# Latent attention: the scores of both softmax maps in one PSUM tile of three banks, and two PSUM tiles for the neighbourhood scores

## The chip, the cores and the metric

One Trainium2 chip, one of its cores. The metric is the device time of one execution of the whole program in microseconds (us); lower is better. The kernel before takes 2817.27 us, the median of three runs (2814.94 to 2818.51).

## What is computed

The program is a network of two blocks over 512 tokens of width 1024. The change is in the second block, which has two layers. In each layer a part of the token width goes through two kinds of attention, with 4 heads of 64 each: a neighbourhood attention (`neighbourhood_attention`: every token sees a window of 8 rows by 16 columns and 256 context tokens) and a latent differential attention, which uses two softmax maps over 512 + 256 keys and subtracts one from the other:

```python
def diff_attend(q1, q2, k1, k2, v, lam):
    scale = DIFF_QK_DIM ** -0.5
    s1 = jnp.einsum('bqhd,bkhd->bhqk', q1, k1).astype(jnp.float32) * scale
    s2 = jnp.einsum('bqhd,bkhd->bhqk', q2, k2).astype(jnp.float32) * scale
    p = jax.nn.softmax(s1, axis=-1) - lam * jax.nn.softmax(s2, axis=-1)
    return jnp.einsum('bhqk,bkhd->bqhd', p.astype(v.dtype), v)
```

`diff_latent` calls it with k1 and k2 made of the 512 rotated keys of the tokens and 256 keys of the context, one block of 128 queries at a time. In the first layer the 256 context tokens also attend to themselves, with 256 keys.

## The kernel before

The kernel is written with a tile framework: the Python code names tiles, and a scheduler decides the order of the instructions on each engine from the program's order and its own costs, and puts in the waits. That order is fixed when the program is built. TensorE (PE), VectorE (DVE), ScalarE (ACT) and the queues of SP and POOL each run their instructions in order.

`attention` (L1653) is one stage per layer. It opens the SBUF tags, replaces the PSUM tags of the matrix products (`GEMM_PS`) by `SOFT_PS`, and runs `units` (L1618): for each of 4 heads and each of 4 query blocks (qb) one neighbourhood unit and one differential unit, 16 pairs a stage. What a unit leaves for later (transposes of the probabilities and the product with the values, `attend_values`, L1409) is run two units later (`AHEAD = 2`). [...] `SOFT_PS` gives `s2` two tiles of 768 columns, which take two banks each, `s1` one tile of one bank, `po` one bank (the products with the values) and `tr` two (transposes).

A differential unit (`differential`, L1501) does for each of two maps: the scores, as two matmuls of 512 and 256 columns into an `s2` tile (L1513); the max over 768 columns on DVE (L1514); the exponential on ACT, which also sums (L1515, recorded under the helper's line L135, tile `ne` for map 0 and `wl` for map 1); the reciprocal of the sum on DVE (L1516). Then DVE combines the maps over 768 columns into `ne` (L1520, helper line L145).

A neighbourhood unit (`neighbour`, L1427) writes 256 columns of context scores into the `s1` tile (L1441, L1442), takes their minimum on DVE (L1445), writes 256 columns of window scores (L1451, L1452), adds the bias and takes the minimum on DVE (L1454), and takes the exponential of 512 columns on ACT (tile `f`, L135).

`attend_values` transposes the probabilities on PE (L1417, tile `tr`), copies them to SBUF (L1421 on ACT, for a part of the neighbourhood units L1419 on DVE) and multiplies with the values on PE (L1423, tile `po`).

In the first layer the same functions also run for the context (`context`, L1642) ahead of the stage, beside matrix products, with 256 keys and the PSUM tag `at` for all scores.

Of the kernel before, what the change touches and what calls it, by code (L numbers as in the profile page):

```python
# [17 lines left out]
P = 128  # L18
# [7 lines left out]
GROUPS = ((128, 1), (512, 4), (2048, 16))  # L26

GEMM_PS = {"mm": 3, "at": 2, "po": 1, "tr": 2}
SOFT_PS = {"s2": 2, "s1": 1, "po": 1, "tr": 2}
BASE = {  # L30
    "wr": 2, "wh": 4, "wl": 4, "f": 5, "h": 2, "acc": 2, "ident": 1, "identr": 1, "ones": 1,
    "rs_y": 4, "rs_t": 2, "rs_v": 2, "rs_v1": 2, "rs_vd": 1, "sil": 2, "adar": 2, "bst": 2, "nb": 2,
# [46 lines left out]
class Net:  # L79
# [1421 lines left out]
    def differential(self, s, yd, ssq, head, qb, qst, kst, vs, c, po):  # L1501
        nc = self.nc
        nk = kst.shape[2]
        cuts = [(k0, min(k0 + 512, nk)) for k0 in range(0, nk, 512)]
        qs = slice(qb * P, (qb + 1) * P)
        sm = self.t([P, 16], "dsm")
        em = []
        for mp in range(2):
            b = mp * 8
            e = self.t([P, nk], self.soft["e"][mp])  # L1510
            ps = self.ps((P, nk), self.soft["s2"])
            for k0, k1 in cuts:
                nc.tensor.matmul(ps[:, k0:k1], lhsT=qst[:, mp, qs], rhs=kst[:, mp, k0:k1], start=True, stop=True)  # L1513
            nc.vector.tensor_reduce(out=sm[:, b + 2:b + 3], in_=ps, axis=AX.X, op=ALU.max, negate=True)  # L1514
            self.act(e, ps, AF.Exp, bias=sm[:, b + 2:b + 3], accum_out=sm[:, b + 3:b + 4])  # L1515
            nc.vector.reciprocal(out=sm[:, b + 6:b + 7], in_=sm[:, b + 3:b + 4])  # L1516
            em.append(e)

        self.stt(sm[:, 15:16], sm[:, 14:15], c["nlam"], sm[:, 3:4], ALU.mult, ALU.mult)
        self.stt(em[0], em[1], sm[:, 15:16], em[0], ALU.mult, ALU.add)  # L1520

        def values():
            o = yd[:, qb, head * 64:(head + 1) * 64]
            self.act(o, self.attend_values(em[0], vs, head, po), scale=sm[:, 6:7])
            junk = self.t([P, 64], "nj")
            self.act(junk, o, AF.Square, accum_out=ssq[:, head, qb:qb + 1])
            if head == 3 and qb == 0 and not s.ctx:
                self.diff_norm(s, yd, ssq, 0, 3)
            if head == 3 and qb == s.nt - 1:
                self.diff_norm(s, yd, ssq, 0 if s.ctx else 3, 4)  # L1530
        return values
# [121 lines left out]
    def attention(self, s, l, c, ne):  # L1653
        self.soft = {"e": ("ne", "wl"), "s2": "s2", "s1": "s1", "pt": "wh"}
        self.open("soft", ne=ne, nsm=5, dsm=5, ssq=2, nj=2)
        self.psum(SOFT_PS)
        po = self.ps((P, 4, P), "po")
        ckv = self.ckv
        vc = [ckv[1][:, i] for i in range(2)]
        vd = [s.kv[3][:, i] for i in range(s.nt)] + [ckv[3][:, i] for i in range(2)]  # L1660
        st, bts = s.st, [self.nbias(l, 0)]

        def more(head):
            bts.append(self.nbias(l, head))
            st.append(self.stacks(s, head))
        todo = [v for v in self.units(s, c, po, st, more, s.kv[1], vc, vd, bts) if v]
        self.gather_start(s)
        for values in todo:
            values()
        self.close("soft")  # L1670
        self.close("heads")
        self.psum(GEMM_PS)
# [249 lines left out]
```

## Time and profile before

| | |
|---|---|
| median of 3 runs | 2817.27 us (2814.94 to 2818.51) |
| profiled execution, its own time | 2815.33 us |
| its span, first to last instruction | 2813.6 us |
| mean granted clock of TensorE | 0.996 of full speed |
| instructions | 38388 |
| first attention stage, from the first scores to the last units | 1452.4 to 1540.9 us of the span |
| second attention stage | 2301.3 to 2388.9 us of the span |

The profile is one execution, recorded by the hardware. All times in it count from the start of its span; the 1.7 us between span and time lie around it. Matmuls are pipelined and their ends are modelled, so the busy time of TensorE is not work at its peak. "PEld" is the loading of a matmul's weights, which runs beside the matmuls before it. Where a helper records an operation, its line is the helper's, so the groups are told apart by their tiles; the profile shows both `s1` and `s2` as `s`.

### The profile page before, as it was taken

To read this page: it belongs to the slowest core of one execution; us is meant where nothing else is said; L and a number is where in the kernel's file an instruction comes from. 1 tells how busy PE (TensorE), PEld (TensorE's weight loads), DVE (VectorE), ACT (ScalarE), POOL (GpSimd) and SP (SyncE) were. 2 spreads that over 40 slices of the span, in tenths; PEclk is the share of its full clock that TensorE was granted. 3 is DMA by queue.
4 is the path that set the end of the run, shared out by engine and by line. 5 is a ranking of instruction groups with operands and counts; after the bars stand their busy time and mean duration, and the time that the engine had idled before them with its cause. 6 is when DMAs were issued, how large, how long until landed. Compare 5 with 4: busy or idle time off the path is not lost.

```text
span 2813.6 us, 38388 instructions
## 1 busy us (share of the span) xinstructions
PE 2750.5 (98%) x15332; PEld 2339.3 (83%) x15332; DVE 1716.7 (61%) x3205; ACT 1057.1 (38%) x1969; POOL 62.4 (2%) x109
## 2 busy tenths in 40 slices
PE   8999999999999999999998999999999999999999
PEld 4888888988888888789887888888888887888887
DVE  6667776453557888787768564444446758644434
ACT  4433433333434222244648232222224547433323
POOL 3000000000020000000000000000000000000000
PEclk9999999999999999999999999999999999999999
DMA  8455344333364555745443411221123443332321
GB/s 275 131 190 173 129 148 141 114 119 105 119 197 135 181 191 192 240 156 174 129 126 79 129 60 60 63 73 61 60 68 106 133 126 90 120 105 90 101 94 60
DMA packets 275203, 354.74 MB, mean 126 GB/s; under 512 B 19320, under 2 KB 221170, under 8 KB 274768
## 3 DMA queue, kind: packets, MB, share of 16 engines
q1 hardware_dynamic: 259744, 323.58, 36.7%
q0 software_dynamic: 4384, 13.99, 1.6%
q10 hardware_dynamic: 10896, 14.72, 1.6%
q8 instruction: 121, 1.98, 0.3%
q14 instruction: 58, 0.48, 0.1%
HBM read 318.62 MB, written 23.65 MB: 122 GB/s over the span
## 4 chain that ended last, share of the span: by engine, by line
PE 82%; DVE 7%; DMA 5%; ACT 3%; issue 2%; POOL 1%; SPq 0%; DVEq 0%; ACTq 0%; POOLq 0%
PE mm L209 24%; PE mm L210 24%; PE mm L211 24%; DMA wr<-in_ada_w 2%; PE po L1423 2%; DVE ada L145 2%; DMA wr<-in_w_ff 2%; DVE wl L138 1%; ACT wh L149 1%; PE at L209 1%; PE tr L1417 1%; PE tr L391 1%; PE at L210 1%; PE at L211 1%; DVE dsm L1514 1%
## 5 line engine op out<-in xcount | busy, mean ns | idle before, releaser
L149 ACT CAST wh<-wr 128x1024 fp32r<-128x1024 f32 (+1 forms) x442 | 425.8, 970 | 842.5 <-PE mm L210 703.8
L138 DVE TENSOR_TENSOR wl<-wr,wh 128x1024 fp32r<-128x1024 f32 (+1 forms) x442 | 494.0, 1122 | 348.6 <-ACT wh L149 339.8
L209 PE MATMUL mm<-h,wh 128*128 128x512 f32 (+1 forms) x1712 | 654.2, 384 | 3.6 <-ACT h L135 2.6
L210 PE MATMUL mm<-h,wh 128*128 128x512 f32 (+1 forms) x1712 | 654.3, 383 | 0.4 <-DVE h L145 0.3
L211 PE MATMUL mm<-h,wl 128*128 128x512 f32 (+1 forms) x1712 | 653.4, 383 | 0.5 <-DVE wl L138 0.5
L209 PEld LDWEIGHTS mm<-h,wh 128*128 128x128 f32 x1712 | 320.9, 188 | 67.6 <-ACT h L135 3.9
L210 PEld LDWEIGHTS mm<-h,wh 128*128 128x128 f32 x1712 | 321.3, 188 | 65.3 <-DVE ada L145 1.7
L211 PEld LDWEIGHTS mm<-h,wl 128*128 128x128 f32 x1712 | 321.6, 188 | 62.6 <-DVE wl L138 0.9
L210 PE MATMUL mm<-mid,wh 128*128 128x512 f32 (+1 forms) x864 | 335.3, 388 | 0.5 <-DVE mid L138 0.5
L209 PE MATMUL mm<-mid,wh 128*128 128x512 f32 (+1 forms) x864 | 335.1, 388 | 0.0
L211 PE MATMUL mm<-mid,wl 128*128 128x512 f32 (+1 forms) x864 | 334.5, 387 | 0.0
L145 DVE SCALAR_TENSOR_TENSOR ada<-wr,cs,ada 128x1024 f32<-128x1024 f32 x168 | 212.6, 1280 | 35.2 <-DMA wr<-in_ada_w 23.9
L135 ACT ACTIVATE f<-mm 128x256 f32<-128x256 f32 (+2 forms) x192 | 99.4, 519 | 260.9 <-PE mm L211 260.6
L209 PE MATMUL mm<-wh,h 128*128 128x256 f32 x704 | 197.4, 281 | 0.0
L210 PE MATMUL mm<-wl,h 128*128 128x256 f32 x704 | 197.2, 280 | 0.0
L211 PE MATMUL mm<-wh,h 128*128 128x256 f32 x704 | 197.0, 280 | 0.0
L210 PEld LDWEIGHTS mm<-mid,wh 128*128 128x128 f32 x864 | 162.5, 188 | 37.1 <-DVE mid L138 1.3
L211 PEld LDWEIGHTS mm<-mid,wl 128*128 128x128 f32 x864 | 162.4, 188 | 36.2
L209 PEld LDWEIGHTS mm<-mid,wh 128*128 128x128 f32 x864 | 162.4, 188 | 35.6
L145 DVE SCALAR_TENSOR_TENSOR x<-mm,modx,x 128x512 f32<-128x512 f32 (+1 forms) x116 | 84.8, 731 | 175.0 <-PE mm L211 172.7
L138 DVE TENSOR_TENSOR f<-f 128x512 f32<-128x512 f32 (+2 forms) x172 | 99.4, 586 | 143.8 <-ACT f L135 142.7
L210 PEld LDWEIGHTS mm<-wl,h 128*128 128x128 f32 x704 | 133.5, 190 | 0.7 <-issue 0.2
(470 smaller groups left out, 4194.0 us busy)
## 6 DMA issues: line engine op xcount, KB each, us to landing
wr<-in_w_ff SPq DMA_DIRECT2D x96, 1024.0 KB
wr<-in_w_in SPq DMA_DIRECT2D x69, 1024.0 KB
wr<-in_ada_w SPq DMA_DIRECT2D x48, 1024.0 KB
wr<-in_w_ada SPq DMA_DIRECT2D x16, 1024.0 KB
wr<-in_w_in SPq DMA_DIRECT2D x24, 512.0 KB
awr<-in_w_ada SPq DMA_DIRECT2D x16, 512.0 KB
wr<-in_w_ret_out SPq DMA_DIRECT2D x8, 1024.0 KB
wr<-in_w_out SPq DMA_DIRECT2D x8, 1024.0 KB
```

The source lines that it names most:

```text
L135: return self.nc.scalar.activation(out=out, in_=in_, func=func, **kw)
L138: return self.nc.vector.tensor_tensor(out=out, in0=a, in1=b, op=op)
L145: return self.nc.vector.scalar_tensor_tensor(out=out, in0=a, scalar=s, in1=b, op0=op0, op1=op1)
L149: self.nc.scalar.copy(hi, src)
L209: mm(out, lhsT=ah, rhs=bh, start=start, stop=False)
L210: mm(out, lhsT=ah, rhs=bl, start=False, stop=False)
L211: mm(out, lhsT=al, rhs=bh, start=False, stop=stop)
L391: when(self.nc.tensor.transpose(ps[:, j], acc[:, m * P:(m + 1) * P], self.ident))
L1417: self.nc.tensor.transpose(tp[:, i], e[:, (b0 + i) * P:(b0 + i + 1) * P], self.ident)
L1423: self.nc.tensor.matmul(po, lhsT=pt[:, kb], rhs=vs[kb][:, head // 2 * P:(head // 2 + 1) * P], start=kb == 0, stop=kb == nk - 1)
L1514: nc.vector.tensor_reduce(out=sm[:, b + 2:b + 3], in_=ps, axis=AX.X, op=ALU.max, negate=True)
```

## The change

`s2` becomes one tile of 1536 columns (three banks), made once a stage and kept in `self.sc`; map 0 has its columns 0 to 767, map 1 the columns 768 to 1535. Map 0's scores are cut at 512, map 1's at 256, so that no matmul crosses a bank: bank 0 holds 512 columns of map 0, bank 1 the last 256 of map 0 and the first 256 of map 1, bank 2 the last 512 of map 1. The bank that this frees goes to a second `s1` tile. The context's own attention keeps its tiles of 256 columns.

```diff
-SOFT_PS = {"s2": 2, "s1": 1, "po": 1, "tr": 2}
+SOFT_PS = {"s2": 1, "s1": 2, "po": 1, "tr": 2}
...
         nk = kst.shape[2]
-        cuts = [(k0, min(k0 + 512, nk)) for k0 in range(0, nk, 512)]
         qs = slice(qb * P, (qb + 1) * P)
...
             e = self.t([P, nk], self.soft["e"][mp])
-            ps = self.ps((P, nk), self.soft["s2"])
+            if s.ctx:
+                ps, cuts = self.ps((P, nk), "at"), ((0, nk),)
+            else:
+
+                ps, cuts = self.sc[:, mp * nk:(mp + 1) * nk], (((0, 512), (512, 768)), ((0, 256), (256, 768)))[mp]
             for k0, k1 in cuts:
...
         po = self.ps((P, 4, P), "po")
+        self.sc = self.ps((P, 1536), "s2")
```

The lines after the first change of `differential` move down by 3 (L1513 becomes L1516, L1514 L1517, L1516 L1519). The scheduler puts the stage in another order. The number behind a tile's name tells one use of it from the next; a name in the waits is the engine whose progress is waited for (Activation is ACT).

On PE, at the scores of the first units of the first stage, before: every map has a tile of its own number, and the tiles 13295 and 13302 (first unit), 13356 and 13363 (second) follow each other in two places in PSUM.

```order
L1513 MATMUL s2_13302<-kst_13127,cqd_13126 128x512 [waits PE_49]
L1513 MATMUL s2_13302<-kst_13127,cqd_13126 128x256
L1451 MATMUL s1_13284<-cqn_13129,cqn_13128 128x256 [waits DVE_49]
L1452 MATMUL s1_13284<-hc_12614,qn_12456 128x256
L1513 MATMUL s2_13356<-kst_13127,cqd_13126 128x512 [waits Activation_49]
L1513 MATMUL s2_13356<-kst_13127,cqd_13126 128x256
L1441 MATMUL s1_13333<-kc_13130,cqn_13128 128x256 [waits Activation_49]
L1442 MATMUL s1_13333<-ckn_11435,qn_12456 128x256
L1417 MATMUL tr_13343<-ident_61,f_13282 128x128 x4
L1513 MATMUL s2_13363<-kst_13127,cqd_13126 128x512 [waits Activation_49]
L1513 MATMUL s2_13363<-kst_13127,cqd_13126 128x256
```

Here the scores of the second unit's map 0 (13356) wait for the exponential of the first unit's map 0, two maps back, and those of its map 1 (13363) for that of the first unit's map 1.

The same engine and place after the change, from the scores of the second unit's map 0 (512, then 256 columns) to those of its map 1 (256, then 512):

```order
L1423 MATMUL po_13277<-hc_12918,wh_13341 128x128 [waits Activation_49]
L1423 MATMUL po_13277<-hc_12918,wh_13341 128x128
L1423 MATMUL po_13277<-cvn_11481,wh_13341 128x128 x2
L1516 MATMUL s2_13278<-kst_13127,cqd_13126 128x512 [waits Activation_49]
L1516 MATMUL s2_13278<-kst_13127,cqd_13126 128x256
L1451 MATMUL s1_13390<-cqn_13129,cqn_13128 128x256 [waits DVE_49]
L1452 MATMUL s1_13390<-hc_12614,qn_12456 128x256
L1451 MATMUL s1_13448<-cqn_13129,cqn_13128 128x256 [waits DVE_49]
L1452 MATMUL s1_13448<-hc_12614,qn_12456 128x256
L1417 MATMUL tr_13369<-ident_61,ne_13295 128x128 [waits DVE_49]
L1516 MATMUL s2_13278<-kst_13127,cqd_13126 128x256 [waits Activation_49]
L1516 MATMUL s2_13278<-kst_13127,cqd_13126 128x512
```

The first wait for Activation at L1516 is for the exponential of the first unit's map 1, the second for that of this unit's map 0: one map back each. The neighbourhood scores (13390 and 13448 are those of the third and fourth units) now come well ahead of their unit.

On DVE, at the third and fourth differential units of the first head after the change (L1519 is the reciprocal, L1517 the max, the last digits of `dsm` name the unit):

```order
L1519 RECIPROCAL dsm_13411<-dsm_13411 128x1 [waits Activation_49]
L1517 TENSOR_REDUCE dsm_13411<-s2_13278 128x1 [waits PE_49]
L1519 RECIPROCAL dsm_13411<-dsm_13411 128x1 [waits Activation_49]
L145 SCALAR_TENSOR_TENSOR dsm_13411<-dsm_13411,lams_9354 128x1 [waits DVE_49]
L145 SCALAR_TENSOR_TENSOR ne_13412<-wl_13418,dsm_13411,ne_13412 128x768 [waits DVE_49]
L1517 TENSOR_REDUCE dsm_13469<-s2_13278 128x1 [waits PE_49]
```

Between the exponential of map 1 (for which the second reciprocal waits) and the max of the next unit stand the reciprocal, the small product and the combination over 768 columns. At the passage to the third unit before the change (unit 13414) the max stood ahead of the combination:

```order
L1516 RECIPROCAL dsm_13354<-dsm_13354 128x1 x2
L1514 TENSOR_REDUCE dsm_13414<-s2_13416 128x1
L145 SCALAR_TENSOR_TENSOR dsm_13354<-dsm_13354,lams_9354 128x1 [waits DVE_49]
L1445 TENSOR_REDUCE nsm_13392<-s1_13393 128x1 [waits PE_49]
L145 SCALAR_TENSOR_TENSOR ne_13355<-wl_13362,dsm_13354,ne_13355 128x768 [waits DVE_49]
```

## Rows read from the trace of the kernel before

**Rows 1.** The page's part 1, whole program: busy us, share, instructions.
```profile
PE 2750.5 (98%) x15332; PEld 2339.3 (83%) x15332; DVE 1716.7 (61%) x3205; ACT 1057.1 (38%) x1969; POOL 62.4 (2%) x109
```
**Rows 2.** Table by stage, both attention stages: length, busy us (instructions), clock, DMA share, GB/s.
```profile
1452.40:1540.90 88.50, 79.53 (x580) 69.72 (x580) 75.74 (x200) 69.27 (x188) 0.00 (x0) 0.98 0.42 101
2301.30:2388.90 87.60, 78.68 (x580) 68.42 (x580) 75.93 (x201) 68.56 (x184) 0.00 (x0) 1.00 0.43 101
```
**Rows 3.** Timeline, start of the first stage: start us, us, instruction, [idle before <-releaser].
```profile
1454.26 0.90 ACT L135 ACTIVATE ne<-s,dsm 128x768 f32<-128x768 f32 x1 [1.70 <-DVE dsm L1514]
...
1455.30 0.30 PEld L1513 LDWEIGHTS s<-kst,cqd 128*128 128x128 f32 x2 [1.69 <-ACT ne L135]
1455.30 0.61 PE L1513 MATMUL s<-kst,cqd 128*128 128x512 f32 x2 [1.48 <-ACT ne L135]
...
1455.95 0.96 DVE L1514 TENSOR_REDUCE dsm<-s 128x1 f32<-128x768 f32 x1 [0.39 <-PE s L1513]
...
1456.21 0.46 PEld L1417 LDWEIGHTS tr<-ident,f 128*128 128x128 f32 x4
...
1456.86 0.67 PE L1513 MATMUL s<-kst,cqd 128*128 128x512 f32 x2
...
1456.95 0.90 ACT L135 ACTIVATE ne<-s,dsm 128x768 f32<-128x768 f32 x1
```
**Rows 4.** Timeline of ACT: last exponential of stage one, first and last of stage two.
```profile
1537.37 0.90 ACT L135 ACTIVATE wl<-s,dsm 128x768 f32<-128x768 f32 x1
...
2303.12 0.90 ACT L135 ACTIVATE ne<-s,dsm 128x768 f32<-128x768 f32 x1 [1.70 <-DVE dsm L1514]
...
2385.43 0.92 ACT L135 ACTIVATE wl<-s,dsm 128x768 f32<-128x768 f32 x1
```
**Rows 5.** Groups by line and shape, 1450 to 1545 us: busy us, mean ns | idle before.
```profile
L1514 DVE TENSOR_REDUCE dsm<-s 128x1 f32<-128x768 f32 x32 | 30.1, 949 | 2.9 <-PE s L1513 2.5
...
L145 DVE SCALAR_TENSOR_TENSOR ne<-wl,dsm,ne 128x768 f32<-128x768 f32 x16 | 16.3, 1016 | 0.3
...
L1421 ACT COPY wh<-tr 128x512 f32<-128x512 f32 x24 | 13.9, 585 | 5.6 <-PE tr L1417 5.6
...
L135 ACT ACTIVATE f<-s,nsm 128x512 f32<-128x512 f32 x16 | 11.0, 685 | 0.3 <-DVE rs_t L138 0.3
...
L1421 ACT COPY wh<-tr 128x256 f32<-128x256 f32 x16 | 6.0, 374 | 2.4 <-PE tr L1417 2.3
L1419 DVE COPY wh<-tr 128x512 f32<-128x512 f32 x8 | 5.5, 685 | 1.0 <-PE tr L1417 1.0
...
L1516 DVE RECIPROCAL dsm<-dsm 128x1 f32<-128x1 f32 x32 | 4.7, 154 | 3.1 <-ACT wl L135 3.0
...
L145 DVE SCALAR_TENSOR_TENSOR dsm<-dsm,lams 128x1 f32<-128x1 f32 x16 | 3.4, 211 | 0.1
```
**Rows 6.** Line L1441 over the whole span: PE's idle time before it (us, times).
```profile
  ACT f L135: 4.0, 10
```
**Rows 7.** Windows, busy us of PE, PEld, DVE, ACT, POOL, then the granted clock, DMA, GB/s.
```profile
1454.00:1455.00 1.00, 0.00 (x0) 0.00 (x0) 1.00 (x4) 0.74 (x1) 0.00 (x0) 1.00 0.86 183
...
1457.00:1458.00 1.00, 1.00 (x5) 0.66 (x5) 0.81 (x3) 1.00 (x3) 0.00 (x0) 0.64 0.86 185
1458.00:1459.00 1.00, 1.00 (x4) 0.90 (x4) 1.00 (x5) 0.86 (x2) 0.00 (x0) 0.50 0.68 146
1459.00:1460.00 1.00, 1.00 (x7) 1.00 (x6) 0.98 (x3) 1.00 (x3) 0.00 (x0) 0.50 0.95 201
1460.00:1461.00 1.00, 1.00 (x7) 0.96 (x6) 0.25 (x2) 0.21 (x2) 0.00 (x0) 0.66 0.35 68
...
2385.00:2390.00 5.00, 3.01 (x23) 2.62 (x24) 4.48 (x9) 2.41 (x8) 0.00 (x0) 1.00 0.50 172
```

## The prediction

> **What bounds the kernel now.** I read the page's busy shares first. Over the whole program TensorE is busy 98% and VectorE 61% [rows 1], but that average is made by the long matrix products, and the change touches only the two attention stages, so the second view is the table by stage [rows 2]. In the 88.5 us of the first stage TensorE is busy 79.5, VectorE 75.7 and ScalarE 69.3 us: 90, 86 and 78%. The second stage (87.6 us) looks the same. No engine rests for long, and none is full. Such a stage is set by how well three queues that each run in order mesh.
>
> The third view is the timeline of one map [rows 3]. A map is one softmax of 128 queries over 768 keys: two matmuls, a max on VectorE, an exponential on ScalarE. Follow one tile: its old exponential ends at 1454.26 + 0.90 = 1455.16; the weight load of the next scores starts at 1455.30; the max starts at 1455.95 and takes 0.96; the exponential starts at 1456.95 and ends at 1457.85. One use of one tile, from exponential end to exponential end, is **2.69 us**. Now there are two tiles: at 1456.86 TensorE writes scores into the one, and 0.09 us later ScalarE starts reading the other. The two 2.69 us chains run beside each other.
>
> The fourth reading is the length of the run of exponentials [rows 3, 4]: from 1454.26 to 1537.37 + 0.90 = 1538.27 is 84.0 us for 32 maps, 2.63 us a map; in the second layer from 2303.12 to 2385.43 + 0.92 = 2386.35 is 83.2 us, 2.60 a map. With two tiles a map may take 5.4 us and the pace still holds, so each map has about 2.6 us in hand to wait in a queue.
>
> **What the change does to this.** It adds and removes no work: 32 maps of 768 columns and 16 neighbourhood units of 512 columns a stage, on the same engines. It cuts the pairs of matmuls of map 1 into 256 and 512 columns instead of 512 and 256, which costs nothing (the same columns). What moves is the waits. Both maps now live in one tile, and the order of TensorE shows it: in the new program the first matmul of map 1 waits for the exponential of map 0 of the same unit, and the first matmul of map 0 of the next unit waits for the exponential of map 1. So one chain runs through all 32 maps of a stage where two ran side by side. Queued behind each such wait on TensorE are transposes and value products; VectorE's max and then ScalarE wait for it.
>
> *The chain alone.* 31 steps of 2.69 plus a last exponential of 0.90 are 84.3 us, against 84.0 and 83.2 now: **+0.3 and +1.1 us**. By itself the chain would just hold the pace. But the 2.6 us in hand are gone, and whatever delays a step now delays the end.
>
> *VectorE's queue.* When an exponential of map 1 ends, VectorE has to do the reciprocal (0.154), the small product (0.211) and the combination of the two maps over 768 columns (1.016) [rows 5]. TensorE needs 0.79 us in the same time for the next scores (1455.16 to 1455.95, [rows 3]). Where the next max stands ahead of the 768-column combination, nothing is lost. Counting the new order of VectorE, at 8 of the 15 passages from unit to unit the combination stands ahead of the max, and at 5 of these a 512-column copy (0.685, [rows 5]) does too. The max then starts 1.38 or 2.07 us after the exponential instead of 0.79: 3 x 0.59 + 5 x 1.28 = **8.2 us a stage**. Three of the eight have a further short instruction in the way; I leave that out against the 0.1 us by which neighbouring instructions overlap in these rows. Today the same order stands in places and costs less, as the max is a tile ahead there.
>
> *ScalarE's queue.* After the exponential of map 0, ScalarE copies the transposed probabilities of an earlier unit (512 columns 0.585, 256 columns 0.374, [rows 5]) before the exponential of map 1. Those transposes stand on TensorE behind the scores of map 1, which wait for the exponential. So the first copy starts after 0.79 plus the four weight loads of the transposes (0.46 for four, [rows 3]), about 1.2 us, and the second ends at 2.15; the max is done at 0.79 + 0.96 + 0.04 = 1.79. The step grows by 0.36. In the new order of ScalarE I count 11 such steps a stage (4.0 us), and three more, after an exponential of either map, where one or two neighbourhood exponentials (0.685) are in the way as well, which I put at 0.8 each: **6.4 us a stage**. This is the least certain term; nothing now shows it. Its lower end is zero (copies may overlap a max that is late anyway), its upper end 16 x 0.96 = 15 us (both copies in full in every step).
>
> *The neighbourhood tiles.* Two tiles let the scores of two or more units run ahead. What that can give is bounded by what TensorE now idles for this tile: 4.0 us over both stages [rows 6]. I cost it at zero: the chain of the maps sets the end, and work done early for the neighbourhood only fills queues earlier. After the last exponential the same instructions follow as now. If the cover were gone, it would be 4 us for the change.
>
> *Sum.* First stage 0.3 + 8.2 + 6.4 = 14.9, second 1.1 + 8.2 + 6.4 = 15.7, together 30.6 us. The profiled execution took 2815.3, so it would take 2845.9. The median of the three runs shown, 2817.3, is 1.9 above it: **2848 us**.
>
> The row of the order has the 512-column matmul of map 0 wait for the exponential of map 1, though the two touch different banks. [...]
>
> **The rivals.**
>
> *The clock falls (chance 0.13).* TensorE will be busy some 80 of 99 us instead of 80 of 88. [...] Against it: in 2385 to 2390 TensorE was busy only 3.01 of 5 us and the clock stayed at 1.00 [rows 7]. [...]
>
> *The queues mesh anyway (chance 0.10).* Only one of the two queue terms shows, because a late max gives the copies time. Then 1.4 + 2 x 8 = 17 us: about 2834.
>
> *Not slower (chance 0.07).* The place is the passage from exponential to next scores. Neighbourhood scores that ran ahead leave VectorE and ScalarE free when the chain wants them, and each step keeps 2.69 us. Then the stages cost +1.4 less up to 4.0 of the neighbourhood's idle time: 2815 to 2819. The point where it decides is the delay per step: below 0.1 us (31 x 0.1 x 2 = 6 us) nothing could be told from no change. For it: VectorE's 75.7 us of work would fit into 84. Against it: the combination of 1.016 us stands in the way at 8 places by the order alone.
>
> *The change does not do what it says.* If the two maps' banks let both chains run beside each other still, there would be no slowdown. The waits in the order exclude it; I give it no chance of its own beyond the last case.
>
> **How the numbers follow.** Forecast as summed, 0.67, own range 2838 to 2860; the clock 0.13; half the queue terms 0.10; not slower 0.07; something unseen, on the high side, 0.03. A range from 2830 to 2870 leaves out the not-slower case, most of the clock's and what is unseen: about 0.2. A change of 0.2%, 5.6 us, is about what a measurement of this kernel can tell from none. Faster by more needs the whole neighbourhood gain and a chain without delays: 0.02. Within 0.2%: 0.05. Slower: 0.93.
>
> **What would show it.** In the profile after, the run of 32 exponentials should take 97 to 101 us a stage. Idle time of TensorE before the scores of a map should name exponentials of the other map and grow from the present few us to over ten, and VectorE's max should wait for TensorE more often. VectorE's share of the stage should fall to about 76%, durations of single instructions staying. Everything outside the two stages should keep its length. The step on VectorE is wrong if the max follows 0.8 us after the exponential at nearly all passages; the step on ScalarE is wrong if it idles before the exponentials of map 1. The prediction is wrong altogether if the run of exponentials stays under 87 us, or if the scores of the next map start before the exponential of the other has ended. A granted clock of 0.9 or less over the stages would mean the first rival.

## The result, and the profile after

The changed kernel takes 2857.37 us, the median of four runs (2850.89 to 2857.78); the kernel before took 2816.55 in the same comparison. The ratio is 1.0141, with a 95% interval of 1.0129 to 1.0154: **slower by 40.8 us**. The profiled execution took 2850.89 us with a span of 2849.1, so it is the quickest of the four.

The page's part 1, beside [rows 1]: the same work on every engine, and a longer span.

```profile
PE 2759.4 (97%) x15332; PEld 2343.2 (82%) x15332; DVE 1722.1 (60%) x3205; ACT 1057.9 (37%) x1969; POOL 62.3 (2%) x109
```

The table by stage answers to [rows 2] (length, busy us of PE, PEld, DVE, ACT and POOL, clock, DMA share, GB/s):

```profile
1448.30:1556.60 108.30, 84.68 (x581) 72.45 (x580) 78.99 (x201) 69.98 (x188) 0.00 (x0) 0.95 0.34 82
2316.60:2423.00 106.40, 83.05 (x581) 71.13 (x580) 79.01 (x201) 68.83 (x184) 0.00 (x0) 0.97 0.35 83
```

The first stage grew by 19.8 us and the second by 18.8. TensorE's share of the stage fell from 90 to 78%, VectorE's from 86 to 73%. The timeline of ACT gives the run of exponentials, as [rows 3, 4] did:

```profile
1450.20 0.90 ACT L135 ACTIVATE ne<-s,dsm 128x768 f32<-128x768 f32 x1 [1.70 <-DVE dsm L1517]
...
1553.12 0.92 ACT L135 ACTIVATE wl<-s,dsm 128x768 f32<-128x768 f32 x1
...
2318.51 0.90 ACT L135 ACTIVATE ne<-s,dsm 128x768 f32<-128x768 f32 x1 [1.70 <-DVE dsm L1517]
...
2419.51 0.92 ACT L135 ACTIVATE wl<-s,dsm 128x768 f32<-128x768 f32 x1
```

From 1450.20 to 1554.04 is 103.8 us (84.0 before), from 2318.51 to 2420.43 is 101.9 us (83.2 before): +19.8 and +18.7, together 38.5. After the last exponential the program takes 428.7 us (2849.1 - 2420.43) against 427.3 before, 1.4 us more; between the two runs it takes 764.5 against 764.9. In this execution the first exponential came 4.1 us earlier than before (1450.20 against 1454.26). These parts add up to the 35.5 us between the two profiled spans (2849.1 - 2813.6); the 40.8 us are between medians. Over the profiled executions of all the kernels here it came between 1450.20 and 1460.29, so a few us of any difference between two executions arise ahead of the stages. The run of exponentials is the finer measure, and I use it beside the times.

The groups by line and shape around the first stage, beside [rows 5]:

```profile
L1517 DVE TENSOR_REDUCE dsm<-s 128x1 f32<-128x768 f32 x32 | 30.6, 955 | 8.0 <-PE s L1516 7.8
...
L1417 PE MATMUL tr<-ident,ne 128*128 128x128 f32 x96 | 16.6, 290 | 13.6 <-DVE ne L145 11.2 <-DVE nsm L1459 2.1
...
L135 ACT ACTIVATE ne<-s,dsm 128x768 f32<-128x768 f32 x16 | 14.5, 906 | 11.3 <-DVE dsm L1517 11.1
L1421 ACT COPY wh<-tr 128x512 f32<-128x512 f32 x24 | 14.1, 585 | 13.3 <-PE tr L1417 13.2
...
L1516 PE MATMUL s<-h 128*128 128x512 f32 x24 | 11.0, 458 | 0.6 <-ACT wl L135 0.6
```

The durations of single instructions stayed (955 against 949 ns for the max, 585 for the copy). The idle time moved: VectorE waits 7.8 us for the scores ahead of the max, where it was 2.5. TensorE waits 13.6 us ahead of the transposes of a combined map, mostly for the combination, and hardly at the scores themselves (0.6 us).

**Where a step loses its time.** A step here is the time from the end of one exponential to the end of the next. By [rows 3] the next max starts 0.79 us after an exponential's end when nothing is in the way (1455.95 - 1455.16). The exponential starts some 0.03 us after the max. I took all 31 steps of a stage from the timeline and noted by how much each max and each exponential came later than that. Seven of the 31 steps in the first stage and eight in the second have no delay and take 2.68 to 2.70 us. The late maxima of the passages from unit to unit are these (us, first and second stage):

```
passage to unit    2     3     4     5     6     7     8     9    10    11    12    13    14    15    16    sum
stage 1         0.01  1.97  0.72  1.85  0.00  1.32  0.00  1.38  1.06  0.91  0.00  1.39  0.01  1.94  0.01  12.6
stage 2         0.01  0.33  0.72  1.92  0.00  1.32  0.00  1.38  1.05  0.92  0.01  1.39  0.01  2.09  0.00  11.2
```

Units 4, 5, 7, 9, 10, 11, 13 and 15 are the eight at which the combination stands ahead of the max in VectorE's order. They hold 10.6 and 10.8 us. Within units the max is late by 2.4 and 1.7 us a stage. Exponentials are late by 4.8 and 4.9 us. With 84.3 for the chain that makes 104.1 and 102.1, against the 103.8 and 101.9 measured. Counted by engine, with what the scores end late put to TensorE first, the max's lateness of 15.0 and 12.9 us is 9.4 and 7.4 for TensorE and 5.5 in either stage for VectorE; the expectations below speak of these.

The passage to unit 7 in the timeline (start, us, instruction), the rows that matter:

```profile
1486.57 0.92 ACT L135 ACTIVATE wl<-s,dsm 128x768 f32<-128x768 f32 x1
...
1487.45 0.61 PE L1423 MATMUL po<-cvd,wh 128*128 128x128 f32 x4
...
1487.90 0.60 PE L1417 MATMUL tr<-ident,f 128*128 128x128 f32 x4
...
1488.06 1.02 DVE L145 SCALAR_TENSOR_TENSOR ne<-wl,dsm,ne 128x768 f32<-128x768 f32 x1
...
1488.26 0.59 PE L1516 MATMUL s<-h 128*128 128x512 f32 x2
...
1489.00 0.68 DVE L1419 COPY wh<-tr 128x512 f32<-128x512 f32 x1
...
1489.60 0.95 DVE L1517 TENSOR_REDUCE dsm<-s 128x1 f32<-128x768 f32 x1
...
1490.58 0.90 ACT L135 ACTIVATE ne<-s,dsm 128x768 f32<-128x768 f32 x1
```

The exponential of map 1 ends at 1487.49. VectorE does the combination (1.02) and a 512-column copy (0.68), and the max starts at 1489.60 instead of 1488.28. TensorE in the same time runs four value products and four transposes; the scores start at 1488.26 instead of 1487.63 and end at 1488.85. Both queues hold the chain up side by side: VectorE's ends last, but the scores alone would have been 0.6 us late.

So it is at all eight. The scores have ended when the max starts, so VectorE comes last; but they end 0.2 to 1.7 us later than in an undelayed step, and by that count TensorE alone would have cost 5.6 and 5.8 us of the 10.6 and 10.8. At four of the eight, VectorE has short instructions in the way beside the combination and the copy. At the passage to unit 11 it is the scaling of a value product, behind the combination; at unit 15 it is three sums of 256 columns ahead of the combination (the last of the three, then the combination):

```profile
1515.74 0.28 DVE L142 TENSOR_SCALAR tok<-po,nsm 128x64 f32<-128x64 f32 x1
1515.93 0.95 DVE L1517 TENSOR_REDUCE dsm<-s 128x1 f32<-128x768 f32 x1
...
1540.66 0.42 DVE L138 TENSOR_TENSOR tok<-tok,rs_y 128x256 f32<-128x256 f32 x1
...
1540.99 1.01 DVE L145 SCALAR_TENSOR_TENSOR ne<-wl,dsm,ne 128x768 f32<-128x768 f32 x1
```

### The profile page after: what moved, and what is told of

It is laid out like the page before. It is cut to its first block, busy times and chain, and to the rows that moved or that the text cites. A ratio compares the mean times of both kernels' runs of the same rounds, so it can differ in the third digit from the quotient of the medians.

```text
span 2849.1 us, 38354 instructions
## 1 busy us (share of the span) xinstructions
PE 2759.4 (97%) x15332; PEld 2343.2 (82%) x15332; DVE 1722.1 (60%) x3205; ACT 1057.9 (37%) x1969; POOL 62.3 (2%) x109
## 3 DMA queue, kind: packets, MB, share of 16 engines
q8 instruction: 120, 1.97, 0.3%
## 4 chain that ended last, share of the span: by engine, by line
PE 83%; DVE 7%; DMA 4%; ACT 3%; issue 2%; POOL 1%; SPq 0%; DVEq 0%; ACTq 0%; POOLq 0%
PE mm L209 25%; PE mm L210 25%; PE mm L211 24%; PE po L1423 2%; DMA wr<-in_ada_w 2%; DVE wl L138 1%; DVE ada L145 1%; PE tr L1417 1%; DMA wr<-in_w_ff 1%; DVE ne L145 1%; ACT wh L149 1%; PE at L209 1%; PE tr L391 1%; ACT wh L1421 1%; PE at L210 1%
```

## Experiments

Twelve kernels ran. Expectations are quoted as they stood before the run; times are medians with the ratio to the kernel before and its interval.

**One tile or the shared bank?** The score tile gets four banks, two for each map, cut as before, and the neighbourhood one tile (the diff is against the changed kernel):

```diff
-SOFT_PS = {"s2": 1, "s1": 2, "po": 1, "tr": 2}
+SOFT_PS = {"s2": 1, "s1": 1, "po": 1, "tr": 2}
...
-                ps, cuts = self.sc[:, mp * nk:(mp + 1) * nk], (((0, 512), (512, 768)), ((0, 256), (256, 768)))[mp]
+                ps, cuts = self.sc[:, mp * 1024:mp * 1024 + nk], ((0, 512), (512, 768))
...
-        self.sc = self.ps((P, 1536), "s2")
+        self.sc = self.ps((P, 2048), "s2")
```

> The scores keep the four banks that they had before (map 0 in columns 0 to 767, map 1 in 1024 to 1791, both cut at 512) and the neighbourhood keeps its one tile; the only difference to the kernel before is that both maps lie in one tile, made once a stage. Theory one tile: the wait goes by the tile, not by the bank, so one chain runs through all 32 maps; the run of exponentials takes 99 to 106 us a stage (84.0 and 83.2 before, 103.8 and 101.9 after the change) and the time is 2848 to 2862 us. Rival shared bank: the serial chain comes from the middle bank that both maps share; with a bank boundary between them two chains run side by side again, 83 to 87 us a stage and 2812 to 2822 us.

Measured: 2860.51 us, ratio 1.0161 [1.0144, 1.0177]. The first and the last exponential of stage one in its timeline:

```profile
1454.22 0.90 ACT L135 ACTIVATE ne<-s,dsm 128x768 f32<-128x768 f32 x1 [1.70 <-DVE dsm L1517]
...
1558.33 0.88 ACT L135 ACTIVATE wl<-s,dsm 128x768 f32<-128x768 f32 x1
```

1454.22 to 1559.21 is 105.0 us, and the second stage has 102.6. With the same banks as before and no bank shared, the chain is as serial as in the changed kernel: no score matmul of a stage starts before the exponential of the map before it has ended, and the earliest starts 0.14 us after that end. In the built program the wait goes by the tile. The three banks and the new cuts are not the cause.

**The second neighbourhood tile.** The change with `"s1": 1`:

> The change with one neighbourhood tile as before (one bank left unused). Theory one tile: the neighbourhood tiles do nothing for the end; 2850 to 2862 us, the run of exponentials 100 to 106 us a stage. Rival early scores: the second neighbourhood tile lets scores of later units stand on TensorE ahead of the scores that the chain waits for, and makes part of the 9.4 and 7.4 us a stage by which TensorE is late; then that lateness falls below 4 us a stage and the time to 2840 to 2849 us. Rival useful tile: the second tile gives time back; without it 2860 to 2868 us.

Measured: 2859.88 us, 1.0156 [1.0141, 1.0171]; 102.5 and 103.3 us a stage. The two runs of exponentials sum to 205.8 us in either kernel, and the intervals overlap: the tile is worth nothing that can be told. TensorE's part of the max's lateness is 6.7 and 7.4 us (9.4 and 7.4 with two tiles), not under the 4 us that the rival of early scores asked for.

**The combination on another engine.** The change, with the combination done on POOL:

```diff
-        self.stt(em[0], em[1], sm[:, 15:16], em[0], ALU.mult, ALU.add)
...
+        else:
+            nc.gpsimd.tensor_scalar(out=em[1], in0=em[1], scalar1=sm[:, 15:16], scalar2=None, op0=ALU.mult)
+            nc.gpsimd.tensor_tensor(out=em[0], in0=em[0], in1=em[1], op=ALU.add)
```

> The change, with the combination of the two maps (16 times 768 columns a stage, 1.01 us each on VectorE) done on POOL in two steps, a product and a sum. Theory VectorE queue: the 5.5 us a stage by which the max starts late after the scores (nearly all of it at the passages to a new unit) goes, as the combination was ahead of it; the run of exponentials falls to 96 to 99 us a stage and the time to 2843 to 2849 us, if the product and sum on POOL (the 512-column sum of the trace takes 1.7 us) are in time for the transposes. Rival copies: the copies of the transposed probabilities on VectorE, not the combination, hold the max up; then the lateness of the max stays above 4 us a stage and the time within 3 us of the changed kernel. Rival late product: POOL is too slow, the transposes of the combined map wait for it and hold TensorE's queue up; slower than 2860 us.

Measured: 2935.54 us, 1.0431 [1.0412, 1.0450]: the rival of the late product. Groups of its first stage:

```profile
L1526 POOL TENSOR_SCALAR wl<-wl,dsm 128x768 f32<-128x768 f32 x16 | 35.8, 2239 | 155.1 <-PE s L1452 87.3 <-DVE dsm L145 63.0 <-PE tr L1417 4.8
...
L1527 POOL TENSOR_TENSOR ne<-ne,wl 128x768 f32<-128x768 f32 x15 | 27.0, 1801 | 1.3
...
L1417 PE MATMUL tr<-ident,ne 128*128 128x128 f32 x90 | 17.6, 327 | 35.8 <-POOL ne L1527 35.8
```

The two steps take 2.24 and 1.80 us, so a combination takes 4.04 us in place of 1.01. TensorE then idles 35.8 us ahead of the transposes of the combined map, and scores queued behind those transposes are late with them. The run says little on VectorE's queue, but it shows how a late operand of work behind the chain reaches the chain through an in-order queue. Part of the loss can be the clock's: over the two runs of exponentials (1453.34 to 1592.11 and 2360.25 to 2500.44) the granted clock was 0.85 in both, where the changed kernel had 0.95 and 0.97 in its own. How much of the 78 us this makes, no run here separates.

The kernel before with the same edit:

> The kernel before, two score tiles, with the same combination on POOL. If the stage before was set by the meshing of three queues, with VectorE busy 75.7 of 88.5 us, taking 16 us a stage off VectorE should shorten the run of exponentials from 84 to some 78 to 82 us a stage: 2805 to 2813 us. If TensorE, busy 79.5 of 88.5 us, sets it, the time stays at 2813 to 2820 us. If POOL is late for the transposes, it is slower than 2822 us.

Measured: 2862.75 us, 1.0163 [1.0148, 1.0179], the last case of the expectation. 46 us lost where the changed kernel loses 78 (2935.54 - 2857.37). That two tiles hide part of the wait is my reading; here the clock fell less as well, to 0.90 and 0.94 over the runs of exponentials.

**The three queues apart.** Three edits of the changed kernel. In `max_before_combine` the combination of a unit is traced after the next unit's first max, with an order edge from that max to it:

```diff
+        ins = self.stt(em[0], em[1], sm[:, 15:16], em[0], ALU.mult, ALU.add)
+        if mx is not None:
+            self.tc.add_manual_dep(ins.ins, mx.ins.name, mybir.DependencyInfo(
+                mybir.DependencyClass.NoSync, mybir.DependencyReason.DATA), reason="max first")
...
+            if mp == 0 and self.held:
+                self.combine(mx)
```

> The change, with each combination of two maps held back on VectorE until the max of the next unit's first map stands ahead of it. Theory VectorE queue: of the 5.5 us a stage by which the max starts late after the scores, only the copies and the short window sums stay, 1 to 2 us; the other delays stay; the run of exponentials is 97 to 100 us a stage and the time 2847 to 2852 us. Rival cover: the late max only hid what TensorE or ScalarE owe anyway, and their lateness grows by as much as that of VectorE falls; 2854 to 2860 us.

In `scores_first` the score matmuls have priority in the scheduler:

```diff
...
+            with self.tc.high_priority():
+                for k0, k1 in cuts:
+                    nc.tensor.matmul(ps[:, k0:k1], lhsT=qst[:, mp, qs], rhs=kst[:, mp, k0:k1], start=True, stop=True)
```

> The change, with the two matmuls of each map's scores given a high priority in the scheduler, so that they go ahead of transposes and value products that are ready in the same moment. Theory TensorE queue: the scores start late because other matmuls were put ahead of them, between the pieces too; the lateness of TensorE (9.4 and 7.4 us a stage) falls below 5 and the time to 2845 to 2852 us. Rival fixed order: the scores become ready while TensorE's queue already holds the others, and priority can't take them back; lateness within 2 us of the changed kernel, 2854 to 2860 us.

In `chain_first` both edits are made, and max and exponential have priority too:

> The change with both: combinations held behind the next max, and scores, max and exponential of every map at high priority. Theory three queues: what the chain owes to TensorE, VectorE and ScalarE together (19.7 and 17.8 us a stage) shrinks to 5 to 10 us; the run of exponentials is 88 to 95 us a stage and the time 2822 to 2842 us, still over the kernel before, as the chain alone takes 84.3. Rival full queues: with TensorE busy some 79 us of a stage there is no slack to win by order; 2848 to 2860 us.

Measured, the lateness worked out from each timeline as above (us, first / second stage):

| kernel | median us, ratio | run of exponentials | max late, passages | max late, within units | exponential late |
|---|---|---|---|---|---|
| the change | 2857.37, 1.0141 [1.0129, 1.0154] | 103.8 / 101.9 | 12.6 / 11.2 | 2.4 / 1.7 | 4.8 / 4.9 |
| `max_before_combine` | 2849.17, 1.0111 [1.0094, 1.0128] | 101.1 / 100.0 | 12.4 / 12.0 | 1.0 / 0.6 | 3.6 / 3.4 |
| `scores_first` | 2855.74, 1.0137 [1.0122, 1.0152] | 102.2 / 103.4 | 10.7 / 10.9 | 2.8 / 3.5 | 4.6 / 4.9 |
| `chain_first` | 2842.80, 1.0092 [1.0077, 1.0107] | 95.7 / 96.8 | 1.1 / 2.3 | 1.7 / 1.7 | 8.8 / 8.8 |

Either edit alone leaves the sum of the passages about where it was, and both together clear them. The passage to unit 7 shows why. With the scores first (scores L1517, max L1518):

```profile
1489.62 0.92 ACT L135 ACTIVATE wl<-s,dsm 128x768 f32<-128x768 f32 x1
...
1490.88 0.60 PE L1517 MATMUL s<-h 128*128 128x512 f32 x2
...
1491.12 1.02 DVE L145 SCALAR_TENSOR_TENSOR ne<-wl,dsm,ne 128x768 f32<-128x768 f32 x1
...
1492.05 0.68 DVE L1419 COPY wh<-tr 128x512 f32<-128x512 f32 x1
...
1492.65 0.95 DVE L1518 TENSOR_REDUCE dsm<-s 128x1 f32<-128x768 f32 x1
```

The exponential ends at 1490.54 and the scores start 0.34 after it, not 0.77; the max still waits for combination and copy and starts 2.11 us after the exponential, as in the changed kernel (1489.60 - 1487.49). With the combination behind the max (scores L1524, max L1525, combination L146):

```profile
1491.65 0.91 ACT L136 ACTIVATE wl<-s,dsm 128x768 f32<-128x768 f32 x1
...
1492.81 0.49 PE L1418 MATMUL tr<-ident,f 128*128 128x128 f32 x3
...
1493.14 0.61 PE L1424 MATMUL po<-cvd,wh 128*128 128x128 f32 x4
...
1493.61 0.59 PE L1524 MATMUL s<-h 128*128 128x512 f32 x2
...
1493.90 0.69 DVE L1420 COPY wh<-tr 128x512 f32<-128x512 f32 x1
...
1494.51 0.95 DVE L1525 TENSOR_REDUCE dsm<-s 128x1 f32<-128x768 f32 x1
...
1495.37 1.01 DVE L146 SCALAR_TENSOR_TENSOR ne<-wl,dsm,ne 128x768 f32<-128x768 f32 x1
```

Now the scheduler has put transposes and value products ahead of the scores: they start 1.05 us after the exponential's end (1492.56). A copy of the transposes stands ahead of the max, which starts 1.95 after it. With both edits (scores L1525, max L1527):

```profile
1489.13 0.90 ACT L136 ACTIVATE wl<-s,dsm 128x768 f32<-128x768 f32 x1
...
1490.25 0.60 PE L1525 MATMUL s<-h 128*128 128x512 f32 x2
...
1490.88 0.96 DVE L1527 TENSOR_REDUCE dsm<-s 128x1 f32<-128x768 f32 x1 [0.32 <-PE s L1525]
...
1492.15 0.88 ACT L136 ACTIVATE ne<-s,dsm 128x768 f32<-128x768 f32 x1
1492.36 1.01 DVE L146 SCALAR_TENSOR_TENSOR ne<-wl,dsm,ne 128x768 f32<-128x768 f32 x1
```

The scores start 0.22 and the max 0.85 us after the exponential's end (1490.03), and the combination comes while the next exponential runs: the step is 3.00 us in place of 3.99.

`max_before_combine` has its median in the forecast range (8.2 us below the changed kernel's), but not for the forecast reason, and its run of exponentials (101.1 and 100.0 us) stays just above the forecast 97 to 100. VectorE's part of the lateness fell from 5.5 to 2.8 and 2.6 us a stage, and TensorE's rose from 9.4 and 7.4 to 10.5 and 9.9: in part what its rival of cover had. It is no clean removal of VectorE's queue, as the order of TensorE changed with it: the passages to units 6, 8, 12, 14 and 16, on time in the changed kernel, are 0.6 to 0.9 us late here. It won within units and on ScalarE, 4.7 us over both runs of exponentials. The other 3.5 us of the medians I can't place, and the two profiled executions took the same (2851.52 against 2850.89). In `scores_first` TensorE's part fell to 4.5 and 5.5 us, but VectorE's stood behind it and rose to 9.0 and 8.9; no gain that its interval shows, and the time lies in the range of its rival. In `chain_first` the passages are clear, and ScalarE's part nearly doubles: 14.6 us are won where 15 to 35 were expected, and the run of exponentials stays above the 88 to 95 us expected. A step of it with a late exponential:

```profile
1469.13 0.96 DVE L1527 TENSOR_REDUCE dsm<-s 128x1 f32<-128x768 f32 x1
...
1469.94 0.86 ACT L1422 COPY wh<-tr 128x512 f32<-128x512 f32 x2 [1.51 <-PE tr L1418]
...
1470.68 0.92 ACT L136 ACTIVATE wl<-s,dsm 128x768 f32<-128x768 f32 x1
```

The max ends at 1470.09; two copies of transposes (0.86 us for both) hold ScalarE until the exponential starts at 1470.68, 0.56 us later than it could. ScalarE was idle for 1.51 us ahead of the copies: they had to wait for the transposes.

**The kernel before, with the same means.** Four score banks and two score tiles again. First the priorities of `chain_first` alone, without the held combination:

> The kernel before with two score tiles, and scores, max and exponential at high priority. Theory: two tiles already cover the queues; the order changes little, 2808 to 2820 us. Rival: the stage before also owed time to the order; the run of exponentials falls below 82 us a stage and the time below 2808 us. Other rival: maps that run ahead push the values and the neighbourhood to the end of the stage; slower than 2820 us.

Measured: 2829.20 us, 1.0043 [1.0026, 1.0059], the last of the three cases. The run of exponentials shrinks in the second stage only (84.6 and 79.3 us, 84.0 and 83.2 before), and there what it overtook comes behind it, on ACT:

```profile
2389.39 0.91 ACT L135 ACTIVATE ne<-s,dsm 128x768 f32<-128x768 f32 x1
...
2399.73 0.69 ACT L135 ACTIVATE f<-s,nsm 128x512 f32<-128x512 f32 x1 [1.50 <-DVE nsm L1454]
```

The last map's exponential starts at 2389.39, the last neighbourhood exponential ten us later. From the end of the last map the program takes 440.7 us (2831.0 - 2390.30), 13.4 more than before.

Then the held combination alone:

> The kernel before (two score tiles) with each combination held behind the next unit's first max on VectorE. Theory cover: with a second tile the max is a tile ahead, and the combination in front of it costs next to nothing, so moving it gives nothing: 2813 to 2822 us. Rival: the combination costs the kernel before as much as the changed one (8 us): 2806 to 2812 us. Other rival: combined maps that come later hold up the transposes: over 2822 us.

Measured: **2811.69 us**, 0.9984 [0.9975, 0.9994], ten runs against nineteen: faster than both kernels, by 5 us of the one and 46 of the other. My theory of cover fell; the time lies in the rival's range, with 5.5 us in place of 8.

```profile
1453.00 0.90 ACT L136 ACTIVATE ne<-s,dsm 128x768 f32<-128x768 f32 x1 [1.70 <-DVE dsm L1522]
...
1534.08 0.91 ACT L136 ACTIVATE wl<-s,dsm 128x768 f32<-128x768 f32 x1
...
2299.60 0.90 ACT L136 ACTIVATE ne<-s,dsm 128x768 f32<-128x768 f32 x1 [1.70 <-DVE dsm L1522]
...
2378.46 0.90 ACT L136 ACTIVATE wl<-s,dsm 128x768 f32<-128x768 f32 x1
```

1453.00 to 1534.99 is 82.0 us and 2299.60 to 2379.36 is 79.8: 2.0 and 3.5 us less than before, which is the whole gain. VectorE's idle time ahead of the max in the first stage is 3.0 us, as before (2.9, [rows 5]). The gain is spread over small waits, and I can't name one that carries it.

**The neighbourhood tile beside two score tiles.** The bank for the second tile is taken from the transposes; the first run measures that alone (`"tr": 1`), the second adds `"s1": 2`:

> The kernel before with one transpose tile in place of two, one bank left unused; the measure for the next run. Transposes of the second half of a map wait for the copy of the first (0.585 us plus what stands ahead of it on ScalarE); 24 maps or units with two copies a stage and two stages give 24 x 2 x 0.6 = 29 us if all of it shows, nothing if the other chain covers it: 2816 to 2846 us.

> As the run with one transpose tile, and the free bank given to a second neighbourhood tile, beside two score tiles. Theory: the neighbourhood tile is worth nothing for the end, within 3 us of the run with one transpose tile. Rival useful tile: it gives the 4.0 us back that TensorE idles for it over both stages, or more: 4 to 10 us faster than that run.

Measured: 2828.00 us, 1.0042 [1.0026, 1.0059], and 2831.96 us, 1.0057 [1.0042, 1.0072]. The lost transpose tile costs 10.8 us. The second neighbourhood tile gives nothing back; 4.0 us slower is just outside what I expected, with overlapping intervals.

**Values one unit later** (`AHEAD = 3` in the kernel before):

> The kernel before with a unit's transposes and value products three units later in place of two. Theory: the order of the queues is set by what is ready, and the stage stays as full as it is: 2812 to 2822 us. Rival: later values leave the queues free for scores: under 2810 us. Other rival: the values pile up at the end of the stage: over 2824 us.

Measured: 2818.59 us, 1.0009 [1.0000, 1.0018]: no difference, as expected.

## Why the prediction was right, and where its sum was short

The forecast was 2848 us with a range of 2830 to 2870; 2857 lies in it, and the sign and the mechanism held. Against its own basis, the profiled execution, the sum gave +30.6 us in the stages. Measured are +38.5, and 1.4 after them.

- **The chain alone, +0.3 and +1.1 us: held.** Steps without delay take 2.68 to 2.70 us, and 2.69 was taken. That one tile makes the chain, whatever its banks, is shown by the run with four banks (105.0 and 102.6 us).
- **VectorE's queue, 8.2 us a stage: the places right, the size short.** The eight passages read from the order are late in both stages; of the other seven only the one to unit 3 is. They cost 10.6 and 10.8 us. Where the step's arithmetic applied it was close: units 4, 7, 9 and 13 took 0.72, 1.32, 1.38 and 1.39 us against 0.59, 1.28, 1.28 and 1.28. One step was too small at the other four: "I leave that out", of the further short instructions. At unit 5 a bias pass (0.49) and a scaling (0.27) stand in the way as well, 1.85 against 1.28; at units 10 and 11 a scaling (0.28), 1.06 and 0.91 against 0.59; at unit 15 three sums of 256 columns (some 0.42 each), 1.94 against 1.28. Another, "TensorE needs 0.79 us in the same time for the next scores", held at none of the eight: the scores end 0.2 to 1.7 us late, at unit 7 because products and transposes of TensorE's own queue come first. That cost nothing more there, as VectorE was later still, but it is why taking VectorE's delay away alone could have won only about half of it.
- **TensorE's queue: no term in the sum.** Outside the eight passages it makes most of the 2.4 and 1.7 us within units and 1.6 of the 2.0 at the passage to unit 3 of the first stage, together 3.8 and 1.7 us (1.6 of it where the clock was low, see the rivals). The prediction named what is queued behind the chain's wait on TensorE, not what stands in front of it. The sum lacks as much here, 5.5 us, as VectorE's term was short of, 5.0.
- **ScalarE's queue, 6.4 us a stage: 4.8 and 4.9.** The exponentials that come late directly behind copies of transposes are 25 in both stages and lose 7.4 us together, 3.7 a stage where 4.0 was taken for 11 of them. Those behind neighbourhood exponentials are two, with 1.6 us together, where 2.4 a stage was taken for three. This term was too large by 1.6 and 1.5 us, mainly in those three.
- **The neighbourhood tiles, zero: held**, by the run with one such tile (205.8 us of exponentials in both).
- **The sum as a sum.** That it came within 8 us of the 38.5 is in part luck, as ScalarE's excess of 3.1 us covers some of the 10.5 that VectorE and TensorE were short of. The terms are not independent either. The queues delay the same steps, so what a term is worth alone can't be read from the total: VectorE's edit left the passages late, TensorE's too, and both together, with max and exponential in front, took 11.4 and 8.9 us off them and gave 4.0 and 3.9 back on ScalarE.

Of the signs, "97 to 101 us" was short by 1 to 3; VectorE's share fell further than the 76% forecast, to 73. "Idle time of TensorE before the scores should name exponentials of the other map and grow to over ten" was wrong: it is 0.6 us at the scores' largest group. TensorE seldom stands at that wait, because it is busy with, or waiting for the operands of, what the order has put in front of the scores; its idle time appears at the transposes of the combined map (13.6 against 1.6 us). VectorE's wait for the scores did grow (7.8 against 2.5 us).

**The rivals.** The clock did fall to 0.50, three times in the first stage (from 1459, 1538 and 1551 us) and twice in the second (from 2405 and 2418), for two or three us each; the kernel before has one such fall in its first stage [rows 7] and none in its second. The windows of the changed kernel (busy us of PE, PEld, DVE, ACT, POOL, clock, DMA, GB/s), shortly after two us in which TensorE was busy 0.50 us together at a clock of 1.00 (1455 to 1457):

```profile
1458.00:1459.00 1.00, 0.52 (x3) 0.31 (x2) 0.73 (x2) 1.00 (x5) 0.00 (x0) 0.88 0.96 207
1459.00:1460.00 1.00, 1.00 (x6) 1.00 (x6) 0.17 (x1) 1.00 (x3) 0.00 (x0) 0.50 0.62 141
...
1461.00:1462.00 1.00, 1.00 (x6) 1.00 (x6) 0.00 (x0) 0.35 (x2) 0.00 (x0) 0.50 0.68 146
1462.00:1463.00 1.00, 0.72 (x5) 0.40 (x3) 0.59 (x1) 0.31 (x2) 0.00 (x0) 0.91 0.89 259
```

From 1459 to 1462 the clock was 0.50. The passage to unit 3 lies there, and is late by 1.97 us in this stage against 0.33 in the other, where the clock was 1.00 at that place (2327 to 2333): 1.6 us. Over the stages the clock was 0.95 and 0.97, not the 0.9 that the rival asked for. That the slowdown does not rest on it is shown by the second run of exponentials of `max_before_combine`:

```profile
2322.34:2422.37 100.03, 79.40 (x567) 67.39 (x568) 74.89 (x193) 68.12 (x180) 0.00 (x0) 1.00 0.36 87
```

The clock was 1.00, and the run still took 100.0 us against 83.2 before. A few us stay open: the other three executions of the changed kernel, 2857.05 to 2857.78 us, had a clock of 0.991 to 0.993 over the whole program, the profiled one 0.995, and where the clock fell in them was not recorded. The rows of the changed kernel show single falls; the run with the combination on POOL had TensorE busy 96.8 of 138.8 us in the first run of exponentials, and a clock of 0.85. The rival with half the queue terms fell, since both showed, 10.6 and 10.8 us at the eight passages and 4.8 and 4.9 on ScalarE. So did "not slower", as only seven and eight of the 31 steps kept 2.69 us.

The wait of a matmul for an exponential of another bank, which the prediction read from the order, is there in the run with four banks as well, where the maps share none: the earliest scores started 0.14 us after the exponential before them had ended, and the runs of exponentials took 105.0 and 102.6 us. What it would give to write map 0's first 512 columns early was not tried; as the wait went by the tile, it would take tiles of one bank and a max and an exponential in pieces.

## What to carry to other kernels

Before two buffers become one, compare the length of one use of the buffer, end to end, with the pace that the stage keeps. Here they were nearly equal (2.69 against 2.63 and 2.60 us), so the chain alone looked free, and what the in-order queues held ahead of its links was then paid for: most of the 38.5 us in the two stages. Count such instructions on each engine of the chain, and take at each step the longest, not one engine's: here VectorE's and TensorE's delays covered each other, so the edits against either alone won 5 us of the two runs of exponentials or nothing, and both together 13. Giving the chain priority only helped until the next queue showed (ScalarE's lateness rose from 4.8 and 4.9 to 8.8 us a stage), and in the kernel before it piled the rest up behind the chain's end (13.4 us more there).

## What was not expected of the hardware and the program

A product of 768 columns with a number per partition took 2.24 us on POOL and the sum 1.80, four times the 1.01 us of VectorE's combination together. Two maps in different banks of one tile made one chain all the same (105.0 and 102.6 us a stage with a bank boundary between them, against 103.8 and 101.9 with a bank shared). And a plain order edge in the kernel before, combination behind the next max, won 5 us that the view of idle times did not announce.
